# Values of the third head group by seven block products on 256 columns in an encoder layer

## The chip, the cores and the metric

The kernel runs on one core of one Trainium2 chip. The time is device microseconds (us) of one execution on that core. Before the change the median of three runs is 2047.3 us, the runs lying between 2046.69 and 2047.52 us. Everything is computed in 32-bit floats; the engines are TensorE (PE, with its weight loads listed apart as PEld), VectorE (DVE), ScalarE (ACT), GpSimd (POOL) and SyncE (SP). In this kernel POOL and SP mainly issue DMAs, each from its own queue in program order.

## The reference

One layer of a bidirectional encoder on x of 1024 positions by 1024 channels:

```python
h = layer_norm(ALPHA * h + 0.5 * swiglu(h, ffn1_w_gate, ffn1_w_up, ffn1_w_down), ln1_g, ln1_b)
h = layer_norm(ALPHA * h + hybrid_mixer(h, ...), ln2_g, ln2_b)
h = layer_norm(ALPHA * h + 0.5 * swiglu(h, ffn2_w_gate, ffn2_w_up, ffn2_w_down), ln3_g, ln3_b)
```

The change lies in the mixer. Its first step is one projection of all positions:

```python
h = x @ w_in + b_in
q, k, v = ...   # 12 heads of 128 channels each
```

The 12 heads are three groups of four. A group attends with its own window and dilation, (128, 1), (512, 4) and (2048, 16); the groups' outputs are combined by their softmax denominators. A Fourier branch and sigmoid gates follow, then an output projection. The values v are a product of 1024 positions x 1024 channels with 1024 x 1536 weights, and each head group has 512 of those 1536 columns.

## The kernel before, in words

**Products.** A 32-bit matrix product is made as three passes of a reduced-precision type: each operand is split into a high and a low part (`split`, L352: the high part by ACT, L358, the low part by DVE, L363), and high x high, high x low and low x high are summed in an accumulator bank (`TERMS`, L343). A bank is 128 partitions x 512 columns; there are eight. Most of the large products are cut into 2 x 2 blocks and made by seven block products in place of eight, after Strassen and Winograd. Line 407 names the operands of each:

```python
PROD = {1: ("a11", "b11"), 2: ("a12", "b21"), 3: ("s4", "b22"), 4: ("a22", "t4"),
        5: ("s1", "t1"), 6: ("s2", "t2"), 7: ("s3", "t3")}
```

The a blocks are the four quarters of the activations (a11 and a12 the first 512 positions, a21 and a22 the last 512; the second index is the half of the channels), s1 to s4 sums and differences of them; the b blocks and t1 to t4 are the same for the weights. `Operand.derive` (L453) makes and splits the activations' side: quarters first, then s1 = a21 - a22, s3 = a11 - a21, s2 = s1 - a11, s4 = a12 + s2, on DVE. An operand is 512 x 512, two pages of 128 x 1024 elements, and its high and low parts take four. SBUF holds 46 such pages and 11 half pages in all; the seven operands of the mixer keep 7 x 4 = 28 pages to the end of its input projection.

**Order.** PE's jobs are a fixed list. All other work (splits, sums, loads, stores) is placed by a planner in the program (`Flow`), which runs through the job list with a cost and a due time for each task, and writes out for every engine one fixed order. Loads are put on SP's queue some 24 us ahead of their job, where pages are free; an operand's splits have due times some 14 us ahead, or 30 us for the activations. Transposes and attention steps are "floats": they slip in between two jobs when their inputs are ready. An engine that waits holds back all that is behind it in its queue. A job of 12 matmuls on 512 columns is the unit.

**Before the value stage.** The first block (a gated feed-forward layer with 21 chunks of gate and up columns, then seven down products) ends with its product 4 (L865). The last four of eight position tiles come out of this product: DVE adds them (L996), ACT and DVE normalise (L1047, L1062), PE transposes (L434), ACT and DVE write the transposed quarters a21 and a22 (L447, L449).

**The value stage.** The values of groups 0 and 1 are one 2 x 2 problem: rows of blocks are the halves of the positions, columns of blocks the two groups. Each product is four jobs, one for each 128 positions. Group 2 is made directly: eight jobs of 24 matmuls, each 128 positions x 512 columns over all 1024 channels. The jobs come as: group 2, tiles 0 to 3; products 1 and 2; group 2, tiles 4 to 7; products 6, 7, 5, 4, 3. Banks: products 1 and 2 add up in A, 6, 7 and 4 in B, 5 and 3 in D (`VORDER`, L1219). Between products DVE reads a bank while it is partly summed, and adds biases (`value_sums`, L1310): t2 after product 6 and t3 after product 7 read bank B before the next product adds to it. Finished tiles are stored to DRAM by POOL (`store_values`). The t weights of groups 0 and 1 are summed in DRAM during the first block: a copy (SP, L1253) and then an accumulating DMA (POOL).

**After it** come 22 pairs of 128-column projections (Fourier channels, queries and keys, gates), with attention slipped in as floats, the branch projections, the output projection, and the second feed-forward block. The output projection also uses seven products; its weight sums are made in DRAM in the same way, at places given by `SUMS0AT` (L1796), which before are tied to the first five jobs of group 2. Attention reads the stored values from DRAM (`load_values`, L1531).

## Time and profile before

| | us |
|---|---|
| median of three runs | 2047.3 |
| the profiled execution | 2046.61 |
| its span, first to last instruction | 2044.8 |
| PE busy | 2033.2 (99%) |
| DVE busy | 1363.2 (67%) |
| ACT busy | 907.1 (44%) |
| POOL busy | 271.5 (13%) |

The granted clock of PE is 0.999 over the span. The profile's page gives busy times, the chain of work that ended last, the costliest groups of instructions and the DMA issues. Further views of the trace give the waits (who waited for whom, total time, times, longest), a timeline, groups of one line's or one tile's instructions (shortest, median and longest duration, first and last start), and windows (busy time and count for each engine, PE's granted clock, the busy share of the 16 DMA engines, GB/s). Tile names follow the code: `Ya221h` is the high part of the mixer's operand a22, second page; `wvt4` the weights t4 of the values; `vB` a bank of the values; `t34a16h` weights t3 and t4 of chunk 16 in the first block ("a"). Matmul records overlap: one lasts from its start to its modelled end, and the next starts before that.

### The profile page before, as it was taken

What the parts mean: (1) busy time and instruction counts of PE and PEld (TensorE: products, weight loads), DVE (VectorE), ACT (ScalarE), POOL (GpSimd) and SP (SyncE); (2) the same over time, 40 slices, a digit from 0 to 9 for tenths busy, and PEclk for the clock granted to TensorE, in tenths of its full rate; (3) what the DMA queues carried; (4) which work ended last, traced back from release to release, by engine and by line L of the source; (5) the groups of instructions that cost most, each with busy time, mean ns of one, the idle gap of its engine ahead of it and who ended that gap; (6) DMA issues with size and microseconds to landing.
All of it is one profiled execution on the core that took longest, in us unless ns stands there. A gap on an engine that the chain in (4) does not pass through costs nothing.

```text
span 2044.8 us, 25909 instructions
## 1 busy us (share of the span) xinstructions
PE 2033.2 (99%) x9387; PEld 1695.7 (83%) x9387; DVE 1363.2 (67%) x1961; ACT 907.1 (44%) x1436; POOL 271.5 (13%) x472
## 2 busy tenths in 40 slices
PE   9999999999999999999999999999999999999998
PEld 7888888888888888888888888888888888888886
DVE  7765655577675668665656666787876665575566
ACT  6433333454553224665556444336533333355332
POOL 0122211111001122231122111000011111110000
PEclk9999999999999999999999999999999999999999
DMA  5779986599957566564445669784257886658752
GB/s 206 235 238 277 296 271 174 171 325 400 312 174 197 178 230 214 188 205 155 114 138 167 229 224 347 266 327 172 77 183 236 270 244 205 194 205 291 240 184 95
DMA packets 173360, 452.71 MB, mean 221 GB/s; under 512 B 20882, under 2 KB 49378, under 8 KB 172720
## 3 DMA queue, kind: packets, MB, share of 16 engines
q1 hardware_dynamic: 126992, 294.70, 41.3%
q0 software_dynamic: 46240, 156.36, 25.6%
q8 instruction: 73, 1.20, 0.2%
q14 instruction: 55, 0.45, 0.1%
HBM read 335.92 MB, written 181.10 MB: 253 GB/s over the span
## 4 chain that ended last, share of the span: by engine, by line
PE 97%; DMA 1%; ACT 1%; DVE 1%; issue 0%; SPq 0%; DVEq 0%; ACTq 0%
PE Ab L496 14%; PE Aa L496 14%; PE Aq L496 8%; PE Db L496 6%; PE Da L496 6%; PE As L496 4%; PE Dq L496 3%; PE Xb L865 3%; PE Zb L865 3%; PE Za L865 3%; PE Xa L865 3%; PE v L1292 2%; PE wA L2277 2%; PE Ds L496 2%; PE vB L1231 2%; PE Va L865 1%
## 5 line engine op out<-in xcount | busy, mean ns | idle before, releaser
L1622 ACT ACTIVATE p<-p,stat 128x192 f32<-128x192 f32 (+2 forms) x96 | 42.2, 441 | 29.7 <-DVE stat L1617 27.7
L338 POOL DMA_DIRECT2D n_spill<-y x16 | 8.7, 547 | 312.1 <-DVE y L1062 311.9
L338 POOL DMA_DIRECT2D hsba<-t2b x21 | 11.5, 550 | 265.3 <-DVE t2b L731 253.6
L338 POOL DMA_DIRECT2D hsaa<-t2a x21 | 11.8, 564 | 258.9 <-DVE t2a L731 258.9
L634 ACT ACTIVATE t2b<-Ab 128x512 f32<-128x512 f32 x21 | 12.6, 598 | 63.8 <-PE Ab L496 63.8
L727 DVE TENSOR_TENSOR t2b<-Db,t2b 128x512 f32<-128x512 f32 x21 | 14.5, 691 | 39.1 <-PE Db L496 39.1
L1412 DVE SCALAR_TENSOR_TENSOR oq<-Dq,b_cols,t2q 128x512 f32<-128x512 f32 x12 | 11.8, 985 | 40.9 <-PE Dq L496 40.9
L634 ACT ACTIVATE t2a<-Aa 128x512 f32<-128x512 f32 x21 | 12.5, 598 | 53.9 <-PE Aa L496 53.9
L1607 DVE SCALAR_TENSOR_TENSOR p<-sc,bias 128x512 f32<-128x512 f32 (+1 forms) x40 | 24.4, 619 | 17.5 <-PE sc L1593 17.1
L727 DVE TENSOR_TENSOR t2a<-Da,t2a 128x512 f32<-128x512 f32 x21 | 14.5, 689 | 31.7 <-PE Da L496 31.7
L1668 PEld LDWEIGHTS pv<-pT,v 128*128 128x128 f32 x240 | 32.4, 191 | 3.3 <-ACT pT L1647 1.0
L1593 PE MATMUL sc<-oq,oq 128*128 128x192 f32 (+2 forms) x192 | 34.4, 322 | 0.0
L719 DVE TENSOR_TENSOR t3a<-Da,t3a 128x512 f32<-128x512 f32 x21 | 14.5, 689 | 28.8 <-PE Da L496 26.2
L1668 PE MATMUL pv<-pT,v 128*128 128x128 f32 x240 | 32.8, 275 | 0.6 <-ACT pT L1647 0.6
L1593 PEld LDWEIGHTS sc<-oq,oq 128*128 128x128 f32 x192 | 29.5, 190 | 1.7
L496 PE MATMUL Da<-Xs40h,usa 128*128 128x512 f32 x84 | 29.3, 389 | 0.0
L496 PE MATMUL Db<-Zs40h,usb 128*128 128x512 f32 x84 | 29.3, 389 | 0.0
L496 PE MATMUL Db<-Zs41h,usb 128*128 128x512 f32 x84 | 29.3, 389 | 0.0
L496 PE MATMUL Da<-Xs41h,usa 128*128 128x512 f32 x84 | 29.3, 389 | 0.0
L719 DVE TENSOR_TENSOR t3b<-Db,t3b 128x512 f32<-128x512 f32 x21 | 14.5, 690 | 22.1 <-PE Db L496 20.0
L1412 DVE SCALAR_TENSOR_TENSOR oq<-Dq,b_cols,t3q 128x512 f32<-128x512 f32 x12 | 11.9, 991 | 23.2 <-PE Dq L496 19.2
L1047 ACT ACTIVATE y<-ya,lsa 128x1024 f32<-128x1024 f32 x8 | 9.1, 1142 | 35.7 <-DVE lsa L1042 35.7
(7599 smaller groups left out, 7366.7 us busy)
## 6 DMA issues: line engine op xcount, KB each, us to landing
qa<-hsas SPq DMA_DIRECT2D x43, 256.0 KB, 5.5
qa<-tdat SPq DMA_DIRECT2D x43, 256.0 KB, 5.4
qb<-hsbs SPq DMA_DIRECT2D x43, 256.0 KB, 4.2
ga<-in_ffn_gu_dram SPq DMA_DIRECT2D x21, 512.0 KB, 7.2
ua<-in_ffn_gu_dram SPq DMA_DIRECT2D x21, 512.0 KB, 8.7
gb<-in_ffn_gu_dram SPq DMA_DIRECT2D x21, 512.0 KB, 5.0
ub<-in_ffn_gu_dram SPq DMA_DIRECT2D x21, 512.0 KB, 6.9
qb<-tdbt SPq DMA_DIRECT2D x33, 256.0 KB, 4.9
```

The lines of the kernel that those rows point to most:

```text
L338: nc.gpsimd.dma_start(*a, **kw)
L496: nc.tensor.matmul(out, pick(w, a)[:, k * P:(k + 1) * P], self.cols(xn, b, k), start=first and k == 0 and ti == 0, stop=last and k == kt - ...
L634: nc.scalar.activation(H[c, t], B[c, "B"], AF.Copy)
L719: nc.vector.tensor_sub(H[c, "t3"], B[c, "D"], H[c, "t3"])
L727: nc.vector.tensor_sub(H[c, "t2"], B.pop((c, "D")), H[c, "t2"])
L865: nc.tensor.matmul(bank_, a, b, start=first and ti == 0, stop=last and ti == len(todo) - 1, skip_group_check=True)
L1231: nc.tensor.matmul(B["v", bk, m], X2.cols(xn, a, k)[:, m * P:(m + 1) * P], pick(w, b), start=new and k == 0 and ti == 0, stop=k == 3 and t ...
L1292: nc.tensor.matmul(ps, X2.cols(f"a{hf + 1}{k // 4 + 1}", a, k % 4)[:, mm * P:(mm + 1) * P], pick(wv, b), start=(k == 0 and ti == 0), stop= ...
L1593: nc.tensor.matmul(sv[:, i, :], qk[0][:, qt * P:(qt + 1) * P], qk[1][:, k0:k0 + w], start=True, stop=True, skip_group_check=True)
L1622: nc.scalar.activation(p3()[:, i, :], p3()[:, i, :], AF.Exp, bias=stats[h][:, k, 0:1], scale=1.0, accum_out=stats[h][:, k, 1:2])
L1668: nc.tensor.matmul(bk[:, at:at + P], env["v"][kc, rows], pt[:, sl * P:(sl + 1) * P], start=not split_ and qt not in seen, stop=last, skip_ ...
L2277: nc.tensor.matmul(B["w", bk, m], X4.cols(xn, a, k)[:, m * P:(m + 1) * P], pick(w, b), start=new and k == 0 and ti == 0, stop=k == 3 and t ...
```

## The change

Group 2 is made by seven block products too. Its 512 columns are cut into two column blocks of 256, so each of its products is four jobs of 12 matmuls on 256 columns. It shares the operands a11 to s4 with the other groups. Its seven weight blocks (four quarters and t1 to t4; one page each, 4 x 256 columns on each partition) are loaded and split as the others are; t1 to t4 are made in DRAM by new copies (SP) and accumulating DMAs (POOL) at chunks 5 to 9 of the first block. Its results are combined on DVE in 32 operations of 256 columns (`third_sums`) with two bias rows, and stored in 16 pieces of 128 x 256.

The order becomes: products 1, 2 and 4 of groups 0 and 1 (product 4 now in a bank set E of its own, read out by a new DVE addition `e21`); products 1 and 2 of group 2; products 5, 6, 7 and 3 of groups 0 and 1; then for position tiles 0 and 1, and again for 2 and 3, products 6, 7, 5, 4 and 3 of group 2. The quarter a21 is no longer split, since only the direct products of group 2 used it. The difference s1 is due at product 5, which now comes before product 6. The weight sums of the output projection move to chunks 16 to 20 of the first block.

```diff
@@ -450,7 +450,7 @@
-        def derive(self, first, whole, lead):
+        def derive(self, first, whole, lead, s1_at=6):
...
@@ -480,7 +480,7 @@
 
                 def s4(i=i):
                     nc.vector.tensor_add(raw["a12", i], raw["a12", i], raw["a11", i])
-                v1 = V(1.23, s1, got["a21", i] + got["a22", i], whole[6], lead + 6, 6.0, pages=1)
+                v1 = V(1.23, s1, got["a21", i] + got["a22", i], whole[s1_at], lead + 6, 6.0 if s1_at == 6 else 2.5, pages=1)
                 v3 = V(1.23, s3, [v1, self.node.get(("a21", i), [])] + list(got["a11", i]), whole[6], lead + 5, 5.0)
                 v2 = V(1.23, s2, [v3, self.node["a11", i]], whole[6], lead + 4, 4.0)
                 parts("s2", i, [v2], whole[6], "a11", 1)
@@ -1216,7 +1216,7 @@
 
     v_d = kb.dram([S0, QW], "v_spill")
     VJ, v_stored, VW, vb, VT = {}, {}, {}, {}, {}
-    VORDER = ((1, "A", True), (2, "A", False), (6, "B", True), (7, "B", False), (5, "D", True), (4, "B", False),
+    VORDER = ((1, "A", True), (2, "A", False), (4, "E", True), (5, "D", True), (6, "B", True), (7, "B", False),
               (3, "D", False))
 
     def value_job(p, bk, new):
@@ -1235,14 +1235,31 @@
         for m in range(4):
             VJ[p, m] = job(12 * MM, product(m), int(new), gives=4 if m == 3 else 0)
 
-    for m in range(4):
-        VJ["g", m] = job(24 * MM, None, 1)
+    TJ = 12 * 0.12
+
+    def third_job(p, m, new, gives=0):
+        def run():
+            bk = VBANK[p]
+            if new:
+                B["t", bk, m] = bank(f"w{bk}{m}")
+            xn, wn = PROD[p]
+            w = [as_k(t, 4) for t in VW["t", wn]]
+            for k in range(4):
+                for ti, (a, b) in enumerate(TERMS):
+                    nc.tensor.matmul(B["t", bk, m][:, :256], X2.cols(xn, a, k)[:, m * P:(m + 1) * P], pick(w, b)[:, k, :],
+                                     start=new and k == 0 and ti == 0, stop=k == 3 and ti == 2, skip_group_check=True)
+        VJ["t", p, m] = job(TJ, run, int(new), gives=gives)
+    VBANK = {p: bk for p, bk, _ in VORDER} | {4: "B"}
     for p, bk, new in VORDER:
         value_job(p, bk, new)
-        if p == 2:
-            for m in range(4, 8):
-                VJ["g", m] = job(24 * MM, None, 1)
-    VJ["g", 7].back["p"] += 12
+        if p == 4:
+            for p_ in (1, 2):
+                for m in range(4):
+                    third_job(p_, m, p_ == 1, 2 if m == 3 else 0)
+    for part in ((0, 1), (2, 3)):
+        for p in (6, 7, 5, 4, 3):
+            for m in part:
+                third_job(p, m, p in (6, 5), 2 if m == 3 else 0)
 
     vblk = {f"b{kh + 1}{g + 1}": in_values[g, 2 * kh:2 * kh + 2] for kh in range(2) for g in range(2)}
     vt = {n: kb.dram([2, P, 1024], f"vt{n}") for n in ("t1", "t2", "t3", "t4")}
@@ -1257,6 +1274,28 @@
         n = Q(J[("a", 1 + i), 4], 1.15, copy, [vtn[x0]] if x0 in vtn else [], lead=0.0)
         vtn[to] = Q(J[("a", 2 + i), 3], 1.6, add, [n], lead=0.0)
 
+    third = in_values[2].rearrange("(h i) p (k c n) -> h c p i k n", h=2, k=2, c=2)
+    tblk = {f"b{kh + 1}{c + 1}": third[kh, c] for kh in range(2) for c in range(2)}
+    tt = {n: kb.dram([P, 1024], f"tt{n}") for n in ("t1", "t2", "t3", "t4")}
+    ttn = {}
+
+    def tile4(t):
+        return t.rearrange("p (i k n) -> p i k n", i=2, k=2)
+    for i, (to, x0, x1) in enumerate((("t1", "b11", "b12"), ("t3", "b12", "b22"), ("t2", "t1", "b22"),
+                                      ("t4", "t2", "b21"))):
+        def copy(to=to, x0=x0):
+            for j in range(2):
+                if x0 in tblk:
+                    nc.sync.dma_start(tile4(tt[to])[:, j], tblk[x0][:, j])
+                elif j == 0:
+                    nc.sync.dma_start(tt[to], tt[x0])
+
+        def add(to=to, x1=x1):
+            for j in range(2):
+                pool_dma(tile4(tt[to])[:, j], tblk[x1][:, j], accum_op=OP.add, max_dma_last_dim=4096)
+        n = Q(J[("a", 5 + i), 4], 0.6, copy, [ttn[x0]] if x0 in ttn else [], lead=0.0)
+        ttn[to] = Q(J[("a", 6 + i), 3], 0.8, add, [n], lead=0.0)
+
     def value_row(key, g, need):
         def run():
             vb[key] = half(f"vb{key}")
@@ -1273,39 +1312,29 @@
     def store_values(t, m, g):
         pool_dma(v_d[m * P:(m + 1) * P, g * 512:(g + 1) * 512], t)
 
-    q2 = value_row(2, 2, VJ["g", 0])
-    for i in range(4):
-        value_part("g2", i, in_values[2, i], (), VJ["g", 0], 14.0)
+    def third_part(n, need):
+        def load():
+            VW["t", n] = t = page(f"wt{n}")
+            if n in tblk:
+                for j in range(2):
+                    nc.sync.dma_start(tile4(t)[:, j], tblk[n][:, j])
+            else:
+                nc.sync.dma_start(t, tt[n])
+        split(f"wt{n}", lambda: VW["t", n], lambda t: VW.__setitem__(("t", n), t),
+              [Q(need, 0.5, load, [ttn[n]] if n in ttn else [], 24.0, pages=1)], need, 14.0)
+
+    for p in PROD:
+        third_part(PROD[p][1], VJ["t", p, 0])
     for p, bk, new in VORDER:
         n = PROD[p][1]
         for i in range(2):
             value_part(n, i, (vblk if n in vblk else vt)[n][i], [vtn[n]] if n in vtn else (), VJ[p, 0], 14.0)
-    for m in range(8):
-        st = {}
-
-        def run(m=m, st=st):
-            hf, mm = divmod(m, 4)
-            st["b"] = ps = bank(f"v{m}")
-            for k in range(KD):
-                wv = [t.rearrange("p (k n) -> p k n", k=2)[:, k % 2, :] for t in VW["g2", k // 2]]
-                for ti, (a, b) in enumerate(TERMS):
-                    nc.tensor.matmul(ps, X2.cols(f"a{hf + 1}{k // 4 + 1}", a, k % 4)[:, mm * P:(mm + 1) * P], pick(wv, b),
-                                     start=(k == 0 and ti == 0), stop=(k == KD - 1 and ti == 2))
-        VJ["g", m].fn = run
-
-        def store(m=m, st=st):
-            t = half(f"vs{m}")
-            nc.vector.tensor_add(t, st["b"], vb[2])
-            store_values(t, m, 2)
-        v_stored[2, m] = V(0.69, store, [VJ["g", m], q2], frees=1, halves=1)
-        fl.later(v_stored[2, m], 3.0, hgives=1 + (m == 7))
-
-    q0, q1 = value_row(0, 0, VJ[1, 0]), value_row(1, 1, VJ[1, 0])
+    q0, q1, q2 = value_row(0, 0, VJ[1, 0]), value_row(1, 1, VJ[1, 0]), value_row(2, 2, VJ["t", 1, 0])
 
     def both_rows():
         vb["s"] = half("vbs")
         nc.vector.tensor_add(vb["s"], vb[0], vb[1])
-    qs = V(0.4, both_rows, [q0, q1], VJ[6, 0], halves=1)
+    qs = V(0.69, both_rows, [q0, q1], VJ[4, 0], halves=1)
 
     def value_sums(m):
 
@@ -1335,8 +1364,11 @@
             nc.vector.tensor_sub(t, B["v", "D", m], page_half("t3"))
             store_values(t, m + 4, 1)
 
+        def e21():
+            nc.vector.tensor_add(page_half("e"), B.pop(("v", "E", m)), vb["s"])
+
         def z21():
-            nc.vector.tensor_add(page_half("t1"), page_half("t1"), vb["s"])
+            nc.vector.tensor_add(page_half("t1"), page_half("t1"), page_half("e"))
 
         def c21():
             t = half(f"v01{m}")
@@ -1354,10 +1386,11 @@
         n1 = V(0.69, t1, [VJ[1, m], q1], VJ[2, m], pages=new_page)
         v_stored[0, m] = V(0.69, c11, [VJ[2, m], n1], frees=1, halves=1)
         n2 = V(0.69, t2, [n1, VJ[6, m]], VJ[7, m], halves=1)
-        n3 = V(0.69, t3, [n2, VJ[7, m]], VJ[4, m], pages=new_page)
+        e = V(0.69, e21, [VJ[4, m], qs], frees=1, pages=new_page)
+        n3 = V(0.69, t3, [n2, VJ[7, m]], VJ[3, m], pages=new_page)
         n4 = v_stored[1, m + 4] = V(0.69, c22, [n3, VJ[5, m]], VJ[3, m], halves=1, gives=m % 2)
-        n5 = V(0.4, z21, [n3, qs])
-        v_stored[0, m + 4] = V(0.69, c21, [n5, VJ[4, m]], frees=1, halves=1, gives=m % 2)
+        n5 = V(0.69, z21, [n3, e], gives=m % 2)
+        v_stored[0, m + 4] = V(0.69, c21, [n5, VJ[7, m]], frees=1, halves=1, gives=m % 2)
         v_stored[1, m] = V(0.69, c12, [n4, VJ[3, m]], frees=int(m > 0))
         if m == 0:
             KT["v", "D"][1] = v_stored[1, m]
@@ -1367,6 +1400,68 @@
     for m in range(4):
         value_sums(m)
 
+    def third_row():
+        vb["t"] = half("vbt")
+        nc.vector.tensor_add(vb["t"][:, :256], vb[2][:, :256], vb[2][:, 256:])
+    qt = V(0.4, third_row, [q2], VJ["t", 6, 0], halves=1)
+
+    def third_sums(m):
+        C, E = slice(0, 256), slice(256, 512)
+        sl = slice(m * 256, (m + 1) * 256)
+        b2, bt = lambda: vb[2], lambda: vb["t"]
+
+        def stored(t, mm, c):
+            pool_dma(v_d[mm * P:(mm + 1) * P, 1024 + c * 256:1024 + (c + 1) * 256], t)
+
+        def t1():
+            if m == 0:
+                VT["w1"], VT["w3"] = page("vw1"), page("vw3")
+            nc.vector.tensor_sub(VT["w1"][:, sl], B["t", "A", m][:, C], b2()[:, E])
+
...
+        def c22():
+            t = VT["h", m][:, E]
+            nc.vector.tensor_sub(t, B["t", "D", m][:, C], VT["w3"][:, sl])
+            stored(t, m + 4, 1)
+
...
+        at = lambda p: VJ["t", p, m]
+        n1 = V(0.42, t1, [at(1), q2], at(2), pages=0 if m else 2)
+        o11 = V(0.42, c11, [at(2), n1], frees=1)
+        n2 = V(0.42, t2, [n1, at(6)], at(7), halves=1)
+        n3 = V(0.42, t3, [n2, at(7), o11], at(4))
+        o22 = V(0.42, c22, [n3, at(5)], at(3))
+        n5 = V(0.42, z21, [n3, qt])
+        o21 = V(0.42, c21, [n5, at(4)], frees=1)
+        o12 = V(0.42, c12, [o22, at(3)], frees=1)
+        v_stored[2, m], v_stored[2, m + 4] = [o11, o12], [o22, o21]
+        fl.later(o12, 3.0, hgives=1)
+        return o22, o21, o12
+    third_ends = [n for m in range(4) for n in third_sums(m)]
+    fl.later(S(0.0, lambda: None, third_ends, hgives=2), 3.0, gives=2)
     S(0.0, lambda: None, [v_stored[0, m] for m in range(4)] + [qs], hgives=2)
     S(0.0, lambda: None, [v_stored[0, m] for m in range(4, 8)], hgives=1)
 
@@ -1377,10 +1472,7 @@
     for i, c in enumerate(pairs):
         PC[c] = (c[0], i)
     pair_run([PC[c] for c in pairs], X2, True)
-    X2.derive({"a11": VJ["g", 0], "a12": VJ["g", 0], "a21": VJ["g", 4], "a22": VJ["g", 4]},
-              {p: VJ[p, 0] for p in PROD}, 30.0)
-    for m in range(8):
-        VJ["g", m].after(*[X2.node[f"a{m // 4 + 1}{kh + 1}", i] for kh in range(2) for i in range(2)])
+    X2.derive({"a11": VJ[1, 0], "a12": VJ[2, 0], "a21": None, "a22": VJ[4, 0]}, {p: VJ[p, 0] for p in PROD}, 30.0, 5)
     for p in PROD:
         VJ[p, 0].after(X2.nodes(PROD[p][0]))
     for c in pairs:
@@ -1565,7 +1657,7 @@
         c = PC["q", idx]
         env = {}
         qv = Q(J[c, 4], 0.5, lambda: env.__setitem__("v", load_values(g, h)),
-               [(v_stored[g, m], 4.0) for m in range(8)], 12.0, pages=1)
+               [(n, 4.0) for m in range(8) for n in (v_stored[g, m] if g == 2 else [v_stored[g, m]])], 12.0, pages=1)
         qb = Q(J[c, 4], 0.1, lambda: env.__setitem__("b", load_bias(g, h)),
                [(shear_n[g * SLOTS + h], 4.0)] + ([bias_done[idx - 2]] if idx >= 2 else []), 12.0)
         if g == 0:
@@ -1793,7 +1885,7 @@
     PW, kept = {}, {}
     oblk = {f"b{kh + 1}{nh + 1}": w_out[2 * kh + nh] for kh in range(2) for nh in range(2)}
     SPREAD = lambda k: 2 * k + 14
-    SUMS0AT = [(VJ["g", i], VJ["g", i + 1]) for i in range(4)]
+    SUMS0AT = [(J[("a", 16 + i), 4], J[("a", 17 + i), 3]) for i in range(4)]
     wt = {n: kb.dram([2, P, 1024], f"wt{n}") for n in ("t1", "t2", "t3", "t4")}
     wtn = {}
 
```

More of the change, by code (lines that the diff above doesn't have):

```diff
@@ L1368, with c11, t2, t3 @@
         value_sums(m)
+    def third_row():
[12 more added lines that the diff above has]
+            nc.vector.tensor_sub(VT["w1"][:, sl], B["t", "A", m][:, C], b2()[:, E])
+        def c11():
+            t = VT["w3"][:, sl]
+            nc.vector.tensor_add(t, B.pop(("t", "A", m))[:, C], b2()[:, C])
+            stored(t, m, 0)
+        def t2():
+            VT["h", m] = t = half(f"vh{m}")
+            nc.vector.tensor_add(t[:, C], B["t", "B", m][:, C], VT["w1"][:, sl])
+        def t3():
+            nc.vector.tensor_add(VT["w3"][:, sl], B["t", "B", m][:, C], VT["w1"][:, sl])
+        def c22():
+            t = VT["h", m][:, E]
+            nc.vector.tensor_sub(t, B["t", "D", m][:, C], VT["w3"][:, sl])
+            stored(t, m + 4, 1)
+        def z21():
+            t = VT["w1"][:, sl]
+            nc.vector.tensor_add(t, t, bt()[:, C])
+        def c21():
+            t = VT["w1"][:, sl]
+            nc.vector.tensor_add(t, B.pop(("t", "B", m))[:, C], t)
+            stored(t, m + 4, 0)
+        def c12():
+            t = VT.pop(("h", m))[:, C]
+            nc.vector.tensor_sub(t, B.pop(("t", "D", m))[:, C], t)
+            stored(t, m, 1)
+        at = lambda p: VJ["t", p, m]
[10 more added lines that the diff above has]
+        return o22, o21, o12
```

## Prediction

> **What bounds the kernel now.** I read the page first (span, busy shares, the chain that ended last), then the waits of PE, then the 123.6 us in which the values are made.
>
> ```profile
> span 2044.8 us, 25909 instructions
> ...
> PE 2033.2 (99%) x9387; PEld 1695.7 (83%) x9387; DVE 1363.2 (67%) x1961; ACT 907.1 (44%) x1436; POOL 271.5 (13%) x472
> ...
> PE 97%; DMA 1%; ACT 1%; DVE 1%; issue 0%; SPq 0%; DVEq 0%; ACTq 0%
> ```
>
> ```profile
> PE warm L2356 <- DVE eps L334: 1.4, 1, 1.4
> PE pD L496 <- DVE pt L2175: 0.9, 1, 0.9
> PE Ds L496 <- DVE t3s L1418: 0.6, 1, 0.6
> PE pv L1668 <- ACT pT L1647: 0.6, 1, 0.6
> PE Aa L496 <- DVE Xa110l L392: 0.2, 1, 0.2
> ```
>
> ```profile
> core 0: us, PE busy (x) PEld busy (x) DVE busy (x) ACT busy (x) POOL busy (x), PEclk, DMA share, GB/s
> 630.00:753.60 123.60, 123.60 (x563) 102.85 (x562) 81.93 (x119) 40.62 (x58) 20.08 (x33) 1.00 0.64 192
> ```
>
> PE is the bound from end to end: it makes 97% of the chain, and its listed waits come to 3.7 us, none of them in the value stage, where it is busy 123.60 of 123.60 us at a granted clock of 1.00 while DVE works 81.93 us (66%). So what shortens PE's own work shortens the kernel, and any new wait of PE lengthens it by its full length. A busy PE can hide idle gaps, so what I count is the pitch, the time from one matmul's start to the next.
>
> **The pitch at 512 and at 256 columns.** First, the 128 matmuls of product 4 of the first block and the bounds of the value stage; then 24 matmuls of 256 columns with a weight load each, from the Fourier part (the second and the last of them), and their loads.
>
> ```profile
> 601.20 0.39 PE L865 MATMUL Ua<-qa40h 128*128 128x512 f32 x1
> ...
> 629.98 0.39 PE L865 MATMUL Ua<-qa410l,qa410h 128*128 128x512 f32 x1
> ```
>
> ```profile
> L1292 PE MATMUL v<-wvg20h,Ya110h x8: 389/389/476, 630.2 to 650.8; 128*128 128x512 f32 x8
> ```
>
> ```profile
> 753.43 0.39 PE L496 MATMUL Au<-Ya110h,gu0h 128*128 128x512 f32 x1
> ```
>
> ```profile
> 1275.68 0.28 PE L2018 MATMUL fp<-posp0l,fold 128*128 128x256 f32 x1
> ...
> 1278.31 0.28 PE L2018 MATMUL fp<-posp1h,fold 128*128 128x256 f32 x1
> ```
>
> ```profile
> L2018 PEld LDWEIGHTS fp<-posp0h,fold x16: 187/190/192, 1275.4 to 1284.5; 128*128 128x128 f32 x16
> ```
>
> 512 columns: (629.98 - 601.20) / 127 = 0.2266 us. 256 columns: (1278.31 - 1275.68) / 22 = 0.1195 us. A single load lasts 0.19 us and still hides at both widths. The value stage runs from 630.2 to 753.43: 123.2 us, of which 528 matmuls x 0.2266 = 119.6 and 3.6 for the 32 transposes slipped in and their switches.
>
> **The change part by part.**
>
> *The third group's products (the gain).* Removed: 8 tiles x 24 = 192 matmuls of 512 columns, 192 x 0.2266 = 43.5 us. Added: 7 products x 4 tiles x 12 = 336 matmuls of 256 columns, 336 x 0.1195 = 40.2 us. Net -3.4 us, all on the path. From below the gain could only grow if the fixed part of a 256-column matmul shrank in long runs: the two pitches give 0.1071 us per 256 columns and 0.0124 fixed, so 336 x 0.1071 = 36.0 and -7.5 us. From above, if the single load's 0.19 us came through as pitch, 336 x 0.19 = 63.8 us and +20.3. I take 0.1195: it is the same type, the same load and the same tile shape.
>
> [...]
>
> *Product 4 of the other groups pulled forward.* It needs the second half's a22, which the last normalised tiles deliver. In the kernel before, that delivery runs so:
>
> ```profile
> 629.05 0.69 DVE L996 SCALAR_TENSOR_TENSOR ya<-Ua,ya 128x512 f32<-128x512 f32 x1 [12.89 <-PE Ua L865]
> ...
> 638.18 0.81 DVE L1062 TENSOR_SCALAR y<-ya,lnrs,lsa 128x1024 f32<-128x1024 f32 x1
> ...
> 643.08 3.92 DVE L449 TENSOR_SCALAR Ya<-tpY,ln_cols 128x128 f32<-128x128 f32 x12 [0.18 <-PE tpY L434]
> ...
> 653.15 1.22 DVE L363 TENSOR_TENSOR Ya221l<-Ya,Ya221h 128x1024 fp32r<-128x1024 f32 x1
> ```
>
> The last tile is normalised at 639.0, turned by 647.0, split at 654.4. In the new order products 1 and 2 (96 x 0.2266 = 21.8 us) and the transposes (3.6) come first, so product 4 starts near 655.6: 1.2 us of cover even if nothing moved. It should move earlier: the four splits of the product-1 and product-2 weights fit into the 12.89 us in which DVE stands idle before 629, the splits of a21 are gone, and a job is now 2.7 us instead of 5.4, so transposes get in sooner. Cost 0; if the cover is gone, the slip shows one for one (a transposition one job later is 2.7 us). The difference s1 is now due a product earlier; it follows the same tiles, 20 us ahead of product 5. The separate bank for product 4 costs 4 additions on DVE; eight accumulators are then in use, but the first four free themselves during product 4's 10.9 us.
>
> *DVE and ACT.* The prices, and the weights' delivery:
>
> ```profile
> L2232 DVE TENSOR_TENSOR prf<-pfe,pfq 128x256 f32<-128x256 f32 x8 | 3.4, 420 | 3.7 <-ACT pfq L2225 3.1 <-PE pfs L496 0.6
> ```
>
> ```profile
> L1298 DVE TENSOR_TENSOR vs<-v,vb 128x512 f32<-128x512 f32 x8 | 5.5, 689 | 17.1 <-PE v L1292 12.4 <-DMA v_spill<-v 4.7
> ```
>
> ```profile
> 647.71 1.12 ACT L358 ACTIVATE Ya220h<-Ya 128x1024 fp32r<-128x1024 f32 x1
> ```
>
> DVE gains 33 additions of 256 columns (33 x 0.42 = 13.9 us) and 4 of 512 (2.8), loses 8 of 512 (5.5), and has 7 weight splits for 4 and two operand splits fewer (+1 x 1.22): +12.4 us. 81.9 + 12.4 = 94 of about 120 us, 79%. ACT gains one split. So on average it is hidden behind PE. Not so in places. In the closing block the jobs last only 12 x 0.1195 = 1.43 us, and product 7 of a tile may start only when DVE has read product 6 of it, one job later. A matmul ends 0.28 us after it starts, 0.16 us into the next job; if DVE has just begun a split of 1.22 us, the 0.42 us read ends 1.80 us into that job, 0.4 us late before any signalling, so nearer 0.5. Four tiles: between 0 and 2 us. Below nothing it can't go, since PE had no wait here to lose. I take 0.8, as DVE is in some operation most of the time but seldom at the start of a long one.
>
> *Queues and transfers.* Moved and added DMAs, from the list of DMA issues, the waits of SP, and the windows of the first block:
>
> ```profile
> vtt<-in_in_values_dram POOLq DMA_DIRECT2D x4, 1024.0 KB, 11.7
> ...
> wtt<-in_out_blocks_dram POOLq DMA_DIRECT2D x4, 1024.0 KB, 11.0
> wvt<-vtt SPq DMA_DIRECT2D x8, 512.0 KB, 5.7
> ...
> v_spill<-v POOLq DMA_DIRECT2D x12, 256.0 KB, 4.8
> ```
>
> ```profile
> SPq L1805 <- DMA wtt<-in_out_blocks_dram: 46.4, 2, 27.0
> ```
>
> ```profile
> 110.00:130.00 20.00, 20.00 (x89) 16.54 (x89) 13.58 (x19) 5.89 (x9) 7.27 (x13) 1.00 0.87 258
> ...
> 150.00:170.00 20.00, 20.00 (x90) 16.57 (x89) 11.85 (x17) 6.55 (x10) 7.15 (x13) 1.00 0.86 257
> 170.00:190.00 20.00, 20.00 (x90) 16.57 (x89) 10.90 (x15) 7.42 (x11) 6.75 (x10) 1.00 0.97 274
> ...
> 210.00:230.00 20.00, 20.00 (x89) 16.54 (x89) 10.89 (x14) 7.41 (x11) 2.63 (x3) 1.00 1.04 287
> ...
> 330.00:350.00 20.00, 20.00 (x90) 16.57 (x89) 9.59 (x13) 7.30 (x11) 1.50 (x2) 1.00 0.75 207
> ```
>
> The chunks of the first block to which sums are tied, by their product 4:
>
> ```profile
> 119.58 0.39 PE L496 MATMUL Aa<-Xa220h,t34a5h 128*128 128x512 f32 x1
> ...
> 194.19 0.39 PE L496 MATMUL Aa<-Xa220h,t34a9h 128*128 128x512 f32 x1
> ...
> 327.47 0.39 PE L496 MATMUL Aa<-Xa220h,t34a16h 128*128 128x512 f32 x1
> ```
>
> The out-weight sums (four copies on SP, four accumulating DMAs on POOL) leave the start of the value stage, where the SP queue stood 46.4 us behind two of them (27.0 the longest), and go to chunks 16 to 20 of the first block, from 327.5 us on and 19 us apart ((194.19 - 119.58) / 4), so an 11.0 us accumulation has landed before the copy that reads it, and the weight loads queued behind that copy on SP aren't held. The copies fall where the DMA share is 0.75. The new sums of the third group (six copies on SP, eight accumulations of half the size on POOL) come at chunks 5 to 9, from 119.6 to some 200 us, where the share is already 0.86 to 0.97 in the windows shown. That is about 1 MB more for each 20 us, beside some 5 MB (257 GB/s x 20 us): the share goes to or past 1, as it is at 210 to 230 with PE busy all 20 us. Cost 0, from a bound of 0 to 1 us; behind it stand loads that are asked for some 24 us ahead. In the value stage the third group's weights take ten issues on SP for four and its stores 16 on POOL for 8, while POOL works 20 of 123.6 us there.
>
> **Sum.** -3.4 + 0.8 = -2.6 us. The profiled execution took 2046.6 us (span 2044.8 and 1.8 around it), 0.7 under the median of 2047.3. The span should come to 2042.2, its execution to 2044.0, the median to 2044.7.
>
> **The rivals.** A measurement here tells about 0.2%, 4.1 us, from no change.
>
> *A. Hand-overs and plan chaos eat more of it.* The closing block needs five weight pairs (ten pages) while 28 of the 46 pages hold the seven operands and two hold sums: six pages are left for raw loads and for the next chunk's weights. A few late splits of 1 to 2 us each make 3 to 7.5 us of waits: 2046.9 to 2051.4. For it: the five deliveries must come 2.9 us apart, where before they were 10.9 apart. DVE also has to wait for a store to land before it reuses a half page; one such wait is the 4.7 us in the row of the 512-column addition. Against it: ACT's 1.1 and DVE's 1.22 us of each fit into 2.9.
>
> *B. Slower: the closing block waits for its weights.* If a weight can be loaded only when a page comes free from the product before, each delivery costs 5.7 (landing) + 1.1 + 1.22 = 8 us against 2.9 of cover: 5 us exposed, for up to five weights 25 us. Two exposed deliveries (10 us) already give 2054; the point is 7.5 us of waits. Against it: products 7 and 3 of the others give back eight pages just before.
>
> *C. Slower: the loads come through at 256 columns.* The 0.19 us pitch above gives 2047.3 + 20.3 = 2067.6. Twenty-four in a row at 0.1195 speak against it; a run of 240 isn't in the trace.
>
> *D. Faster: the fixed part shrinks in the long run.* -7.5 + 0.8 gives 2040.6, and any mixture of it counts as faster beyond 4.1. [...]
>
> *E. The sums stay hidden but the gain is given back later.* PE has no wait after the stage that the earlier end would lengthen; each later transfer hangs on PE's progress. It would give 2047.3.
>
> **How the numbers follow.** My forecast, waits of 0 to 2.5 us: 0.62, 2043.2 to 2046.4. A: 0.16. E: 0.02. B: 0.11, C: 0.01, together slower 0.12. D: 0.03; the few waits of PE elsewhere (3.7 us listed) falling better in the re-planned order: 0.05; together faster 0.08. A and E stay inside 0.2%, so same is 0.80. Range: 2043.0 leaves out most of D, 2049.5 holds half of A and leaves out B and C: 0.2 in all.
>
> **What would show it.** Right: the new matmuls at a pitch of 0.12 over the whole closing block; the value stage 119.8 us from first matmul to the first of the next; waits of PE on DVE of some tenths between products 6 and 7 of the third group; none ahead of product 4; SP no longer held for the out-weight sums. Wrong: a pitch above 0.1295 (43.5 / 336, where the gain is gone); a PE wait on an a22 split or on a weight split; DVE over 90% in the closing block; PE waits before 630 us from the fuller DMA share.

## The result, and the profile after

The median fell from 2047.18 us (2046.28 to 2048.34, 20 runs) to 2043.68 us (2043.05 to 2044.53, 20 runs): a ratio of 0.9983, with a 95% interval of 0.9977 to 0.999, or 3.5 us less. The forecast was 2044.7 us, 2.6 us less, with a chance of 0.80 that the change would stay inside 0.2%; it came to 0.17%.

The page of the kernel after, with its span, the busy time of the engines and the shares of the chain that ended last:

```profile
span 2041.9 us, 26284 instructions
...
PE 2030.3 (99%) x9531; PEld 1700.4 (83%) x9531; DVE 1373.7 (67%) x1991; ACT 908.4 (44%) x1437; POOL 284.6 (14%) x488
...
PE 97%; DMA 1%; ACT 1%; DVE 1%; issue 0%; SPq 0%; DVEq 0%; ACTq 0%
```

PE issues 144 more matmuls (336 - 192) and is busy 2.9 us less; the span is 2.9 us shorter (2044.8 to 2041.9). The list of PE's waits of the kernel after (line waited for: us in total, times, longest):

```profile
PE warm L2448 <- DVE eps L334: 1.4, 1, 1.4
PE pD L496 <- DVE pt L2267: 0.9, 1, 0.9
PE Ds L496 <- DVE t3s L1510: 0.6, 1, 0.6
PE pv L1760 <- ACT pT L1739: 0.6, 1, 0.6
PE Aa L496 <- DVE Xa110l L392: 0.2, 1, 0.2
```

They are the five of before, 3.7 us in all; none lies in the value stage. (The line numbers differ because lines were added above them.) The whole stage and then its closing block, in the view of windows (the first figure of a row is the length of the window):

```profile
core 0: us, PE busy (x) PEld busy (x) DVE busy (x) ACT busy (x) POOL busy (x), PEclk, DMA share, GB/s
630.00:750.30 120.30, 120.30 (x707) 106.95 (x706) 95.90 (x152) 44.19 (x61) 22.29 (x40) 1.00 0.50 170
720.00:750.00 30.00, 30.00 (x246) 29.73 (x246) 18.95 (x35) 5.05 (x6) 8.79 (x17) 1.00 0.59 203
```

PE is busy all the time at a granted clock of 1.00. DVE works 95.9 of 120.3 us, 80% where 79% was forecast, and only 63% in the closing block. The weight loads of PE, however, fill 29.73 of 30 us there; an experiment below asks what that means. PE's timeline gives the pitch: the first matmul of the stage, the first of the closing run, its last, and the first of the next stage.

```profile
630.15 0.39 PE L1231 MATMUL vA<-wvb110h,Ya110h 128*128 128x512 f32 x1
...
721.42 0.28 PE L1249 MATMUL wB<-wtt2h,Ys20h 128*128 128x256 f32 x1
...
750.10 0.28 PE L1249 MATMUL wD<-wtb22h,Ys41l 128*128 128x256 f32 x1
750.22 0.40 PE L496 MATMUL Au<-Ya110h,gu0h 128*128 128x512 f32 x1
```

The 240 matmuls of the closing run take 750.22 - 721.42 = 28.80 us, 0.1200 us each; the row of 24 from the Fourier part had said 0.1195. The stage lasts 750.22 - 630.15 = 120.1 us, 3.1 less than the 123.2 of before, and 192 x 0.2266 - 336 x 0.1200 = 43.5 - 40.3 = 3.2 us. So the difference is PE's own matmul time in this stage, and nothing was lost to waits. Nor was it given back later: PE's last matmul in the kernel before, and then in the kernel after, starts 3.09 us earlier.

```profile
2036.82 0.39 PE L865 MATMUL Ub<-qbb5l,qsb3h 128*128 128x512 f32 x1
```

```profile
2033.73 0.39 PE L865 MATMUL Ub<-qbb5l,qsb3h 128*128 128x512 f32 x1
```

The span is only 2.9 us shorter; the 0.2 us between lie behind PE's last matmul.

### The profile page after: what moved, and what is told of

It is laid out like the page before. It is cut to its first block, busy times and chain, and to the rows that moved or that the text cites. A ratio compares the mean times of both kernels' runs of the same rounds, so it can differ in the third digit from the quotient of the medians.

```text
span 2041.9 us, 26284 instructions
## 1 busy us (share of the span) xinstructions
PE 2030.3 (99%) x9531; PEld 1700.4 (83%) x9531; DVE 1373.7 (67%) x1991; ACT 908.4 (44%) x1437; POOL 284.6 (14%) x488
## 4 chain that ended last, share of the span: by engine, by line
PE 97%; DMA 1%; ACT 1%; DVE 1%; issue 0%; SPq 0%; DVEq 0%; ACTq 0%
PE Ab L496 14%; PE Aa L496 14%; PE Aq L496 8%; PE Db L496 6%; PE Da L496 6%; PE As L496 4%; PE Dq L496 3%; PE Xb L865 3%; PE Zb L865 3%; PE Za L865 3%; PE Xa L865 3%; PE wA L2369 2%; PE Ds L496 2%; PE Va L865 1%; PE Vb L865 1%; PE Yb L865 1%
## 5 line engine op out<-in xcount | busy, mean ns | idle before, releaser
L1709 DVE TENSOR_REDUCE stat<-p 128x2 f32<-128x384 f32 (+2 forms) x40 | 24.3, 618 | 1.0
L634 ACT ACTIVATE t3a<-Aa 128x512 f32<-128x512 f32 x21 | 12.5, 597 | 26.7 <-PE Aa L496 26.6
```

Source lines behind the costliest of these rows:

```text
L634: nc.scalar.activation(H[c, t], B[c, "B"], AF.Copy)
L1709: nc.vector.tensor_reduce(stats[h][:, cols, 0], p3(), AX.X, OP.max, negate=True)
```

## The experiments

All times are medians; each ratio is to the kernel before, run beside it, with its 95% interval. "Against after" is the difference to 2043.68 us. The median of the kernel before lay between 2046.84 and 2047.18 us from one set of runs to the next, so a difference of a few tenths in the last column says nothing. The last two rows rest on two executions each.

| kernel | us | ratio | against after |
|---|---|---|---|
| out-weight sums moved, nothing else | 2047.14 | 1.0 (0.999 to 1.001) | +3.5 |
| after, sums back in the value stage | 2049.02 | 1.001 (1.0 to 1.002) | +5.3 |
| after, product 4 back behind 7 | 2043.62 | 0.9981 (0.9972 to 0.9991) | -0.1 |
| after, product 4 second | 2052.18 | 1.0024 (1.0014 to 1.0034) | +8.5 |
| after, closing block tile by tile | 2046.82 | 0.9999 (0.9989 to 1.0008) | +3.1 |
| after, 112 third-group matmuls more | 2057.30 | 1.0051 (1.0034 to 1.0068) | +13.6 |
| after, 672 matmuls of 128 columns for 336 | 2078.34 | 1.0153 (1.0136 to 1.017) | +34.7 |
| after, 672 matmuls added, small loads | 2085.10 | 1.0185 (1.0156 to 1.0215) | +41.4 |
| after, 672 matmuls added, full loads | 2118.67 | 1.0349 (1.0319 to 1.0379) | +75.0 |

**The out-weight sums alone.** One line of the change, made on the kernel before:

```
-    SUMS0AT = [(VJ["g", i], VJ["g", i + 1]) for i in range(4)]
+    SUMS0AT = [(J[("a", 16 + i), 4], J[("a", 17 + i), 3]) for i in range(4)]
```

> The kernel before with one part of the change: the weight sums of the output projection move from the start of the value stage to chunks 16 to 20 of the first block. My theory (the gain is PE's own work, PE has no wait in the value stage): no change, 2047.2 within 0.5 us, and PE's listed waits stay the five of before, 3.7 us. The rival (the 46.4 us that SP stood behind these sums cost something, or the sums disturb the first block): faster by 0.5 to 2 us, or slower by as much through a PE wait between 327 and 420 us.

Measured: 2047.14 us, no different from before. Without the new order the sums cost nothing in either place, though the SP queue stood 46.4 us behind two of them in the value stage.

**The change without the move of the sums.** The kernel after, with the four sums back in the value stage, spread over its first products:

```
-    SUMS0AT = [(J[("a", 16 + i), 4], J[("a", 17 + i), 3]) for i in range(4)]
+    SUMS0AT = [(VJ[1, 0], VJ[1, 2]), (VJ[1, 2], VJ[2, 0]), (VJ[2, 0], VJ[2, 2]), (VJ[2, 2], VJ[4, 0])]
```

> The changed kernel with that one part undone: the weight sums of the output projection stay in the value stage, tied to the jobs of products 1, 2 and 4, 5.4 us apart as before. My theory: the sums fit there too, 2043.7 within 0.7 us, with SP held by them for 20 to 50 us. The rival (the sums had to go, because SP is now needed there for the weights of product 5 and of the third group): a wait of PE on a weight split between 666 and 690 us, 2 to 10 us, so 2046 to 2054.

Measured: 2049.02 us, 5.3 us over after and 1.8 over before. The theory failed and its rival came true: here the move is worth more than the products. The place is in PE's waits of this kernel:

```profile
PE vD L1231 <- DVE wvt10l L363: 3.7, 1, 3.7
```

The weights of product 5 come late. They are queued on SP behind a copy (L1897) that had to wait for an accumulation. SP's wait and its timeline in this kernel, and then the issue of the same six loads in the kernel after:

```profile
SPq L1897 <- DMA wtt<-in_out_blocks_dram: 26.7, 1, 26.7
```

```profile
658.54 0.53 SPq L1897 DMA_DIRECT2D wtt<-wtt  x1
659.17 8.35 SPq L1308 DMA_DIRECT2D wvt<-vtt  x6
```

```profile
636.58 36.23 SPq L1308 DMA_DIRECT2D wvt<-vtt  x6
```

22.6 us of lead are gone. How the late load reached PE is seen on ACT and on DVE of this kernel:

```profile
668.05 1.04 ACT L358 ACTIVATE wvt10h<-wvt 128x1024 fp32r<-128x1024 f32 x1
```

```profile
678.64 2.35 DVE L482 TENSOR_TENSOR Ya<-Ya,Ya 128x1024 f32<-128x1024 f32 x2
680.91 1.21 DVE L363 TENSOR_TENSOR wvt10l<-wvt,wvt10h 128x1024 fp32r<-128x1024 f32 x1
```

By 668 the weights were on the chip, 10 us before product 5 was due at 678.04, but DVE's split of them stands at 680.91, behind other work in the order written out beforehand (in the kernel after it ran at 667.32). The late issue and the place in DVE's order changed together here, so how much each would cost alone stays open. The wait cost more than its length; that is taken up at the end.

**Product 4 back in its old place.** The pull-forward alone is undone: product 4 follows 7 in bank B, without the extra bank and its four additions. The core of the edit:

```
-VORDER = ((1, "A", True), (2, "A", False), (4, "E", True), (5, "D", True), (6, "B", True), (7, "B", False),
+VORDER = ((1, "A", True), (2, "A", False), (5, "D", True), (6, "B", True), (7, "B", False), (4, "B", False),
...
-        if p == 4:
+        if p == 2:
```

> The changed kernel with product 4 of groups 0 and 1 back where it was, after product 7 and in bank B, without its own bank and without the four additions for it; the third group's products 1 and 2 then follow product 2. My theory (the pull forward moves PE's work and takes none away): 2043.7 within 1 us. The rival (it makes room before the closing block, because banks, pages and DVE time come free earlier): PE waits in or just before the closing block, 1 to 5 us more, 2045 to 2049.

Measured: 2043.62 us, the time of after. The pull-forward neither brings nor costs anything, and the first products of the third group find their operands and weights in time without it.

**Product 4 one place earlier still.** How thin the cover in front of it is:

```
-VORDER = ((1, "A", True), (2, "A", False), (4, "E", True), (5, "D", True), ...
+VORDER = ((1, "A", True), (4, "E", True), (2, "A", False), (5, "D", True), ...
...
-        if p == 4:
+        if p == 2:
```

> The changed kernel with product 4 of groups 0 and 1 one place earlier still, right after product 1, and product 2 behind it: this takes away 10.9 us of the cover between the first block and the first use of a22. In the changed kernel the splits of a22 end at 654.6 us and product 4 starts at 655.5. My theory (only the cover hides the delivery): product 4 would be ready to start at about 645, the splits can come forward by a few us at most since the last tile is normalised at 638.9, so PE waits 3 to 10 us on a split of a22: 2046.7 to 2053.7, more where the clock falls after the wait. The rival (the delivery isn't tight, its place in the order follows the due time): no wait, 2043.7 within 0.7 us.

Measured: 2052.18 us, 8.5 over after. PE's waits of this kernel show the two that are new, and its timeline where they fall:

```profile
PE vE L1231 <- ACT Ya220h L358: 5.2, 1, 5.2
...
PE vE L1231 <- DVE Ya220l L363: 0.6, 1, 0.6
```

```profile
650.37 0.80 PE L1231 MATMUL vE<-wvt40h,Ya220h 128*128 128x512 f32 x1 [5.18 <-ACT Ya220h L358]
...
652.19 0.79 PE L1231 MATMUL vE<-wvt40h,Ya220l 128*128 128x512 f32 x1 [0.59 <-DVE Ya220l L363]
```

The theory held, and the a22 splits are indeed what bounds product 4 from the front: product 2's 10.9 us are its cover.

**The closing block tile by tile.** In the kernel after, the products of two tiles alternate, so that one other job (1.44 us) lies between product 6 and product 7 of a tile. Here that job is taken away:

```
-    for part in ((0, 1), (2, 3)):
+    for part in ((0,), (1,), (2,), (3,)):
```

> The changed kernel with the closing block tile by tile: products 6, 7, 5, 4, 3 of tile 0, then of tile 1, 2 and 3, so no job lies between product 6 and product 7 of a tile. My theory (the hand-over takes some 0.16 us of matmul end, 0.42 us of DVE read and some signalling, and one job of 1.43 us covers it): four waits of PE on DVE of about 0.7 us, up to 1.9 us where DVE has begun a split; 3 to 7 us in all, 2046.5 to 2050.7. The rival (PE does not wait for the read, or another wait hides it): 2043.7 within 0.7 us.

Measured: 2046.82 us, 3.1 over after; the gain of the change is gone. PE's waits and the first of the four hand-overs, on PE and on DVE:

```profile
PE wB L1249 <- DVE vh L1428: 2.2, 4, 0.6
```

```profile
722.48 0.28 PE L1249 MATMUL wB<-wtt2h,Ys21l 128*128 128x256 f32 x1
723.37 0.35 PE L1249 MATMUL wB<-wtt3h,Ys30h 128*128 128x256 f32 x1 [0.61 <-DVE vh L1428]
```

```profile
722.80 0.42 DVE L1428 TENSOR_TENSOR vh<-wB,vw 128x256 f32<-128x256 f32 x1 [0.44 <-PE wB L1249]
```

From start to start it takes 0.89 us where 0.12 is the pitch: 0.77 us lost although DVE stood idle and began at once. Of these, 0.42 is the read, 0.15 passes from its end (723.22) to the start on PE, and the other 0.20 is the tail of the last matmul and the start of the read. Over the four tiles the starts are 2.8 us further apart than the pitch, of the 3.1 measured. In the same kernel one job lies between products 7 and 4, and between 5 and 3, which share a bank too: PE has no wait at any of these eight hand-overs.

In the kernel after, DVE's timeline at the same hand-over shows how the alternation covers it:

```profile
722.23 1.22 DVE L363 TENSOR_TENSOR wtt4l<-wtt,wtt4h 128x1024 fp32r<-128x1024 f32 x1
723.37 0.42 DVE L1428 TENSOR_TENSOR vh<-wB,vw 128x256 f32<-128x256 f32 x1
723.70 1.22 DVE L363 TENSOR_TENSOR wtb22l<-wtb,wtb22h 128x1024 fp32r<-128x1024 f32 x1
```

Product 6 of tile 0 is done at 721.42 + 11 x 0.12 + 0.28 = 723.02. DVE is in a weight split then, so the read ends only at 723.79; product 7 of the tile is due at 721.42 + 24 x 0.12 = 724.30, and 0.5 us are left, of which the step from the read's end to PE takes some 0.15.

**More of the same matmuls.** The third term of each product is issued once more, 112 matmuls in all, so the values of the third group change in this kernel and only the time is read:

```
+                    if ti == 2:
+                        nc.tensor.matmul(B["t", bk, m][:, :256], X2.cols(xn, a, k)[:, m * P:(m + 1) * P], pick(w, b)[:, k, :],
+                                         start=False, stop=k == 3, skip_group_check=True)
```

> The changed kernel with the last of the three passes of every third-group product made twice (448 matmuls of 256 columns in place of 336; the extra pass changes the third group's values, so what is timed is the matmuls' price). My theory (0.1195 to 0.12 us for each, with no fixed saving in a long run): 112 x 0.12 = 13.4 us more, 2057.1 within 0.7. The rival with a shrinking fixed part: 112 x 0.107 = 12.0, 2055.7. If the closing block were bound by DVE or by weights, less than 10 us more would show, since the others would use the time.

Measured: 13.6 us over after, 13.6 / 112 = 0.1216 us each. In PE's timeline the closing run, now 320 long, goes from here to here:

```profile
724.91 0.28 PE L1249 MATMUL wB<-wtt2h,Ys20h 128*128 128x256 f32 x1
...
763.30 0.40 PE L496 MATMUL Au<-Ya110h,gu0h 128*128 128x512 f32 x1
```

38.39 / 320 = 0.1200 us. A longer run doesn't get cheaper and nothing else hid the cost: one matmul of 256 columns with its load is 0.12 us of the kernel's time.

**Half the columns.** Each matmul of the third group is cut in two of 128 columns, each with its own load:

```
-                    nc.tensor.matmul(B["t", bk, m][:, :256], ..., pick(w, b)[:, k, :], ...)
+                    for c in range(2):
+                        nc.tensor.matmul(B["t", bk, m][:, c * P:(c + 1) * P], ..., pick(w, b)[:, k, c * P:(c + 1) * P], ...)
```

> The changed kernel with each 256-column matmul of the third group cut into two of 128 columns, each with its own weight load: 672 in place of 336, nothing else moved. If the pitch is the stream plus a fixed part (0.0535 per 128 columns + 0.0124): 0.066 us, 672 x 0.066 = 44.3 us, 4 us more, 2047.7. If the single load of 0.19 us came through whole: 672 x 0.19 = 127.7, 2131. [...]

Measured: 34.7 us over after. The closing run in PE's timeline has 480 matmuls between these two rows:

```profile
731.07 0.33 PE L1250 MATMUL wB<-wtt2h,Ys20h 128*128 128x128 f32 x2
...
784.62 0.45 PE L496 MATMUL Au<-Ya110h,gu0h 128*128 128x512 f32 x1
```

53.55 / 480 = 0.1116 us: half the columns take 93% of the time. Neither expected time was met: 2047.7 lies 30.6 us too low, 2131 lies 53 us too high. By the pitches, 672 x 0.1116 - 336 x 0.1200 = 34.7 us, the measured difference. Something other than the columns sets the pitch here.

**Is it the load?** Behind each job of the kernel after, 24 matmuls of 128 columns are added, into the unused half of its banks, once with a load of 64 columns (`nw = 64`) and once with one of 128 (`nw = 128`). Only the time of the added matmuls is read; with the full load the kernel's output changes too (a relative error of 0.0256), though nothing reads their columns, and no run shows why:

```
+            for j in range(24):
+                nc.tensor.matmul(B["t", bk, m][:nw, 256:256 + P], X2.cols(xn, "hi", 0)[:, m * P:m * P + nw],
+                                 pick(w, "hi")[:, 0, :P], start=True, stop=True, skip_group_check=True)
```

> The same 672 extra matmuls of 128 columns, but with a weight load of 64 columns (128 x 64) in place of 128, so only half of the output partitions. My theory (the pitch of 0.1116 us at 128 columns is the weight load, which takes about half as long for 64 columns, and then the stream of 0.066 us decides): 672 x 0.066 = 44 us more, 2088, within 4. The rival (0.1116 us is the least distance of two such matmuls, whatever is loaded): 75 us more, 2118.7.

> The changed kernel with 24 extra matmuls behind each of the 28 third-group jobs, 672 in all: a full weight load (128 x 128) and 128 columns each, written to the unused columns of the job's bank and never read. In the run with halved width a 128-column matmul came at a pitch of 0.1116 us. If that pitch is general: 672 x 0.1116 = 75 us more, 2118.7. By the stream plus the fixed part of 0.066 us: 44 us more, 2088.

Measured: 41.4 / 672 = 0.0616 us for each with the small load, 75.0 / 672 = 0.1116 with the full one. PE's timeline agrees; between the starts of two neighbouring groups lie 24 added matmuls and one job of 1.44 us. First with small, then with full loads:

```profile
734.50 1.60 PE L1252 MATMUL wB<-wtt2h,Ys20h 128*64 128x128 f32 x24
...
737.42 1.60 PE L1252 MATMUL wB<-wtt2h,Ys20h 128*64 128x128 f32 x24
```

```profile
743.79 2.79 PE L1252 MATMUL wB<-wtt2h,Ys20h 128*128 128x128 f32 x24
...
747.91 2.79 PE L1252 MATMUL wB<-wtt2h,Ys20h 128*128 128x128 f32 x24
```

(2.92 - 1.44) / 24 = 0.0617 and (4.12 - 1.44) / 24 = 0.1117 us. The time expected from the theory of the small load came (41.4 us, 44 expected), and 0.1116 us is the pitch of other matmuls of 128 columns too. With the small load the pitch is 55% of that with the full one; the load itself is recorded as 0.135 us against 0.192, 70% and not about half. The moving operand is the same; the load has half the columns, and with them half the rows are written. The runs don't part these two, but it isn't the columns streamed that make 0.1117 us at 128 columns; the load is the likelier. If so, the author's estimate from these two pitches is that 0.1117 us is a floor for matmuls with a load of 128 columns, and the new ones, at 0.1200, stand 0.008 us above it; fewer than 128 columns weren't tried. The 29.73 of 30 us of the closing block don't show this by themselves: loads that are recorded as 0.19 us and start 0.12 us apart overlap in the record, so the row looks full without being the limit.

## Why the prediction was right, point by point

- **The gain.** Forecast -3.4 us; the pitches of after give -3.2, the stage -3.1, the two profiled spans -2.9, the medians -3.5. The step held, and so did its choice of the 0.1195 us row over its ends: rival C (the load's 0.19 us comes through) and rival D (0.1071 us in a long run) both fall with 0.1200 over 240 and over 320 in a row. The run with more of the same shows that such a matmul costs its pitch in the kernel's time (0.1216 us by the medians, 0.1200 by the timeline). The 0.3 us between -3.2 and -3.5 are within what medians of the same kernel differ by.
- **The hand-over in the closing block** is the term that was mis-sized: 0.8 us forecast, from 0 to 2; measured 0. The mechanism is there. With no job between, a hand-over costs 0.7 us each; with one of 1.44 us between and DVE in a weight split of 1.22 us, 0.5 us are left. The forecast's 0.4 us of lateness belongs to a split that begins just as product 6 ends; here the split had begun 0.8 us earlier. Whether a split begins at the worse moment is settled by the planner's order, which the prediction didn't work out. This term is most of the 1.0 us by which the forecast lay too high.
- **Product 4.** "Cost 0" held, and undoing the pull-forward moved nothing. But the step said that the delivery of a22 "should move earlier", with the four splits of the product-1 and product-2 weights inside DVE's idle time before 629. It didn't. DVE in the kernel after, the first product-2 split, the last copies of transposes and the last split of a22, and then PE at the last transposes and where product 4 begins:

```profile
631.93 1.22 DVE L363 TENSOR_TENSOR wvb210l<-wvb,wvb210h 128x1024 fp32r<-128x1024 f32 x1
...
647.51 1.37 DVE L449 TENSOR_SCALAR Ya<-tpY,ln_cols 128x128 f32<-128x128 f32 x4 [0.18 <-PE tpY L434]
...
653.40 1.22 DVE L363 TENSOR_TENSOR Ya221l<-Ya,Ya221h 128x1024 fp32r<-128x1024 f32 x1
```

```profile
646.43 1.04 PE L434 MATMUL tpY<-ident,y 128*128 128x128 f32 x8
...
655.49 0.39 PE L1231 MATMUL vE<-wvt40h,Ya220h 128*128 128x512 f32 x1
```

  Only the product-1 splits ran ahead of 629 (from 609.07 on). The product-2 splits ran after it, the last transposes were copied by 648.9 us against 647.0 before, and a22 was complete at 654.6 against 654.4. Product 4 began at 655.49, so the cover was 0.9 us, less than the 1.2 counted on without any move. So the cost was 0 by that narrow margin and not for the reason given, and that far it was luck. Product 4 in second place shows what the missing cover costs: 5.8 us of waits, and 8.5 us in all.
- **DVE** took 80% of the stage (79% forecast) and hid behind PE. The seven weight blocks that it splits are three quarters (b11, b21 and b22, not four) and t1 to t4; b12 enters only through t1 and t3.
- **The out-weight sums.** "Cost 0" was right for the change as a whole, and alone the move does nothing. What the step left out is the other side: in the new order the sums can't stay in the value stage as they were tried here, since a copy that waits on SP (26.7 us) holds the weight loads behind it (issued 22.6 us later). The forecast saw that queue ("aren't held") and didn't price what it would cost if it were kept: 5.3 us, more than the whole gain. The sign "SP no longer held" came in the main: in the kernel after SP waits 5.3 us once for these accumulations, where it had waited 46.4. They landed later than counted on, in 15.2 us (median) instead of 11.0. A hold of SP is not a loss by itself: one of the third group's new copies held it for 23.8 us in the first block, and PE had no wait there.
- **DMA in the first block.** The share went past 1, as forecast, and cost nothing. Three windows of the kernel after at the third group's sums, and one where the moved out-weight sums fall:

```profile
150.00:170.00 20.00, 20.00 (x90) 16.58 (x89) 11.84 (x17) 6.61 (x10) 8.29 (x13) 1.00 1.03 270
170.00:190.00 20.00, 20.00 (x90) 16.57 (x89) 10.14 (x14) 6.90 (x10) 9.36 (x14) 1.00 1.04 273
190.00:210.00 20.00, 20.00 (x90) 16.54 (x89) 11.80 (x19) 6.52 (x10) 6.87 (x10) 1.00 1.05 308
...
330.00:350.00 20.00, 20.00 (x90) 16.57 (x89) 9.65 (x13) 7.29 (x11) 2.43 (x3) 1.00 1.04 318
```

  PE is busy 20 of 20 us in each. The last of them had a share of 0.75 before, and the forecast didn't add to it what it moved there.
- **Rivals A and B** (hand-overs and late weights in the closing block) didn't come: PE has no wait there. The last weight split, `wtb22l`, ends at 724.92, when the closing run is 3.5 us old. **E** (given back later) fell too: PE's waits after the stage are those of before, and its last matmul starts 3.1 us earlier.
- **Two figures of the prediction** don't follow from its own terms, and neither changes the forecast. With no wait its sum gives 2047.3 - 3.4 = 2043.9, not the 2043.2 at which its band begins, which lacks the 0.7 us from the profiled execution to the median. The stage of 119.8 us that it names as a sign leaves out the 0.8 for hand-overs; with it the stage is 120.6, and 120.1 was measured.

## What to carry to other kernels

Where PE doesn't wait, as in this stage, the sum of count times pitch is a good forecast (3.4 us, and 3.5 measured), provided the pitch is taken for the same type, load and width. Cutting columns paid here from 512 to 256 (0.2266 us to 0.1200) and no longer from 256 to 128 (0.1200 to 0.1116), where something else, most likely the weight load, set the pitch. The gain must then still survive the hand-overs, since shorter jobs cover less: one job of 1.44 us between a product and the next into the same bank was enough here, none was not (0.7 us lost each time). A move that does nothing by itself can be what a larger change stands on, so each part of a change is worth trying both alone and taken out of the whole. A queue that issues in order deserves a price for the case in which its waiting entry stays where it was (5.3 us here).

## What the runs showed of the hardware that was not expected

**A long wait of PE cost more than its length.** After the 3.74 us wait in the kernel with the sums back, PE's matmuls of 512 columns start 0.43 us apart instead of 0.2266, as its timeline shows; the windows of the same kernel give the granted clock (the last number but two):

```profile
682.97 0.63 PE L1231 MATMUL vD<-wvt10h,Ys10h 128*128 128x512 f32 x1
683.40 0.63 PE L1231 MATMUL vD<-wvt10l,Ys10h 128*128 128x512 f32 x1
```

```profile
682.00:686.00 4.00, 3.83 (x10) 3.01 (x11) 4.00 (x5) 1.19 (x2) 0.00 (x0) 0.57 0.00 0
686.00:690.00 4.00, 4.00 (x19) 3.30 (x18) 1.80 (x2) 1.06 (x1) 0.00 (x0) 1.00 0.77 223
```

About nine matmuls run so, 0.2 us more each: 3.7 + 1.8 = 5.5 us, which is the difference of the two spans (2047.4 - 2041.9). With product 4 second, where 5.2 and 0.6 us of waits come close together, the windows show it for longer:

```profile
652.00:656.00 4.00, 3.81 (x9) 3.04 (x10) 2.41 (x3) 3.62 (x5) 0.00 (x0) 0.50 0.40 131
```

By the medians the waits came to 1.4 and 1.5 times their length (5.3 us for 3.7, 8.5 for 5.8); the waits of 0.6 us in the tile-by-tile kernel left its mean clock at 0.999. In the row above the granted clock is 0.50, and the matmuls start at about twice the pitch (0.43 us). After the shorter wait the slow matmuls last some 3.5 us (682.17 to 685.7). After the longer one they last from 650.37 to 657.5, about 7 us with the 0.6 us wait among them; why it is twice as long isn't shown, nor how long a wait must be for it.

**The load's recorded duration isn't its pitch.** A load of 128 columns is recorded as 0.19 us, as this row from the full-load kernel shows, and yet the added matmuls there, each with its load, have a pitch of 0.1117 us (its columns: ns min, median, max):

```profile
L1252 PEld LDWEIGHTS wA<-wtb11h,Ya110h x96: 192/192/192, 667.1 to 682.1; 128*128 128x128 f32 x96
```

It holds at 256 columns too: in the kernel after, with every load and matmul of the closing run marked 128*128, loads recorded as 0.19 us fit under a pitch of 0.1200 us over 240 matmuls.
